# Two transformer blocks on one core: the rests of the ordinary weight tiles from ScalarE and an accumulating DMA instead of VectorE

## The chip, the cores and the metric

One Trainium2 chip, one core. The core's engines run side by side, each through its own list of instructions in order, and wait for each other through semaphores: TensorE (PE) multiplies, VectorE (DVE), ScalarE (ACT) and GpSimd (POOL) work elementwise, SyncE (SP) issues most of the DMAs; 16 DMA engines move the data. The metric is the device time of one execution in microseconds (us); lower is better.

## The reference

Two layers, one after the other, on 512 tokens of width 1024, all in f32. Cut to the large products:

```python
def first_block(x, c, ...):
    mod = silu_c @ ada_w[l] + ada_b[l]
    h = rms_norm(h_res, norm_pre_w[l]) * (1.0 + scale) + shift
    z = h @ w_in[l]                          # 1024 -> 6144
    u_pool, g_pool, q, f_pre, i_in, g_h = jnp.split(z, ...)
    pool_out = multiscale_pool(u_pool, pool_w[l], pool_scale[l]) * jax.nn.silu(g_pool)
    o = hgrn2_chunkwise(q, log_f, k, i_in)
    y = jnp.concatenate([pool_out, hgrn_out], axis=-1) @ w_out[l]
    h_res = h_res + gate * rms_norm(y, norm_post_w[l])
...
def hybrid_layer(x, norm_g, w_in, ...):
    proj = rms_norm_2(x, norm_g) @ w_in      # 1024 -> 11208
    y_a = chunked_spatial_gating(...); y_b = dsa_attention(...)
    y_c = short_gated_conv(...);       y_d = forgetting_attention(...)
    branch_d = jnp.einsum('nbsw,nwd->bsnd', ys, w_branch)
    merged = jnp.sum(jax.nn.sigmoid(gates) * branch_d, axis=2)
    return x + merged @ w_out
```

Each weight is read once from DRAM, and nearly all of the arithmetic is products of the 512 tokens with a weight.

## The kernel before

**Products in three parts.** TensorE multiplies in a rounded f32 format (f32r). To keep the precision, an operand is split into a rounded part and a rest: `whi` and `wlo` for a weight, `HH` and `HL` for the tokens. A product is three products, `HH·whi + HH·wlo + HL·whi`, in one PSUM bank; the list of each tile begins with `whi`, and the first product with `wlo` comes second or third (`mm3`, line 334). One product of 128x128 with 128x512 follows the last after about 0.23 us.

**Weight tiles.** The packed weights `wts` are loaded by SP, 1 MB at a time (two tiles of 128x1024), into the three raw buffers (`dma_raw`, line 237), and near the end also into groups of slots of 128x512. `pump` (line 280) splits the next tile: ScalarE rounds it into `whi` (line 308), VectorE subtracts `whi` from the raw weights and writes `wlo` (line 309). When both tiles of a raw buffer are split, the buffer is free (`used`, line 253) and SP's next load is issued. There are 188 tiles in the ring:

- eight `s` tiles at the start (896 columns),
- 42 `P` tiles (`P1n2_0` and the like) in the last quarter, products of a Strassen scheme, whose weights are sums made in the buffers (`prep`, line 263),
- 138 ordinary tiles: `q3`, `i0_0`, `f4`, `u0`, `gp0`, `ki`, `dq0`, `gt0_1_0`, `wb2_0_0` and so on. Each is read by 24 products, some 5.4 us of TensorE; a `P` tile by 12, some 2.7 us.

**The ring.** `whi` and `wlo` have three buffers each (`WB = 3`), used in turn, and a tile is asked for two tiles ahead (`LA = 2`). So the split of a tile can begin when the tile three places earlier has had its last product, and has to end when the two tiles between them are done. Between two tiles the side work puts its own products (`hgrn`, `topk`, `fox`, `dsa`: attention and scans, stepped by `run`, line 817).

**What sets the order.** A scheduler orders each engine's list at build time from priorities; the splits have high priority (line 305). On the chip the lists are fixed, and each engine takes its instructions in that order. Eight startup steps (to line 543) are ordered by hand on VectorE and ScalarE. ScalarE also evaluates all functions and copies most banks out (helper `act`, line 110). GpSimd has only `HL` at the start (line 522), a factor per `f` tile (line 568) and the running sums of the pooling windows, up to four chained additions for each `u` tile (lines 915 to 921); after the first 330 us it is nearly empty. Before the change it issues no DMA. At the two last steps of a branch in the last quarter come the `wb` tiles: `P7n2_0`, `P7n2_1`, `wb2_1_0`, `wb2_1_1`, then `P2`, `P4`, `wb2_0_0`, `wb2_0_1`, the same for branches 3 and 1.

Of the kernel before, what the change touches and what calls it, by code (L numbers as in the profile page):

```python
# [13 lines left out]
AF = mybir.ActivationFunctionType  # L14
ALU = mybir.AluOpType
# [73 lines left out]
def kernel(  # L89
# [15 lines left out]
    V, A, G, T = nc.vector, nc.scalar, nc.gpsimd, nc.tensor  # L105
# [23 lines left out]
    def get():  # L129
        assert free_slots, "out of slots"  # L130
        s = Slot(free_slots.popleft())
        low[0] = min(low[0], len(free_slots))
        return s
# [7 lines left out]
    def bget():  # L141
        assert banks, "out of banks"
        return banks.popleft()
# [40 lines left out]
    whi = [const.tile([128, 1024], F32R, name=f"whi{i}") for i in range(WB)]  # L184
    wlo = [const.tile([128, 1024], F32R, name=f"wlo{i}") for i in range(WB)]
# [4 lines left out]
    for r, items in enumerate(raws):  # L190
        o = 0
        for name, w in items:
            if name[0] == "B":
                quarter[name[1:]] = r
                n, q = name[1:].split("_")
# [9 lines left out]
    n = 0  # L205
# [27 lines left out]
    def width(w, *bufs):  # L233

        return w if all(b.t is not None for b in bufs) else 512
# [17 lines left out]
    def used(r):  # L253
        left[r] -= 1
        if left[r] == 0:
            b = raw_b.pop(r)
            if ws["dma"] >= len(raws) and b.s:
                put(*b.s)
            else:
                pool.append(b)  # L260
                dma_raw()

    def prep(i):

        if i >= len(flat) or flat[i][0][0] != "P":
            return
        p, n, j = flat[i][0][1], flat[i][0][3], int(flat[i][0][5])
        args = {"5": ("11", "12"), "6": ("11", "22"), "7": ("12", "22"), "4": ("11", "21")}.get(p)
        if args is None:
            return  # L270
        rd, ra = (quarter[f"{n}_{q}"] for q in args)
        d, a_ = raw_b[rd], raw_b[ra]
        w = width(1024, d, a_)
        for o in range(j * 1024, (j + 1) * 1024, w):
            with tc.high_priority():
                V.tensor_sub(d.at(o, w), a_.at(o, w), d.at(o, w))
        if p in "74":
            used(ra)

    def pump(upto):  # L280
        while ws["split"] <= min(upto, len(flat) - 1):
            i = ws["split"]
            name, r, o, w = flat[i]
            if i in in_slots:
                hs, ls = [get(), get()], [get(), get()]
                for kk in range(2):
                    src = raw_b[r].at(o + kk * 512, 512)
                    with tc.high_priority():
                        A.activation(hs[kk].r, src, AF.Copy)
                        V.tensor_sub(ls[kk].r, src, hs[kk].r)  # L290
                in_slots[i] = hs, ls
                used(r)
                ws["split"] += 1
                continue
            if i not in split_ids:
                if i >= ws["next"]:
                    return
                ws["split"] += 1
                continue
            while ws["prep"] <= i + 1:  # L300
                prep(ws["prep"])
                ws["prep"] += 1
            s = split_ids[i] % WB
            b = raw_b[r]
            with tc.high_priority():
                n = width(w, b)
                for c in range(0, w, n):
                    A.activation(whi[s][:, c:c + n], b.at(o + c, n), AF.Copy)  # L308
                    V.tensor_sub(wlo[s][:, c:c + n], b.at(o + c, n), whi[s][:, c:c + n])  # L309
            used(r)  # L310
            ws["split"] += 1

    def wget(name, ahead=LA):
        i = ws["next"]
        assert flat[i][0] == name, (flat[i][0], name)
        ws["next"] += 1
        pump(i + ahead)
        if i in in_slots:
            return in_slots[i]
        s = split_ids[i] % WB  # L320
        return whi[s], wlo[s]
# [109 lines left out]
    for h in range(2):  # L431
        r = slice(32 * h, 32 * h + 1)
# [4 lines left out]
    for h in range(2):  # L437
        r = slice(32 * h, 32 * h + 1)
# [55 lines left out]
    for k in range(8):  # L494
# [3 lines left out]
        for i in range(1, 4):  # L498
# [4 lines left out]
        V.tensor_scalar(S1[:, kc], md[:, 1:2], B1[:, kc], PV[:, PV_NPW + k:PV_NPW + k + 1],  # L503
                        op0=ALU.add, op1=ALU.mult)
        pump(k)
        xk = xnT[k].f if k else xb[0][:]
        if k == 0:
# [685 lines left out]
    w = {}  # L1193
    first = ws["next"]
    for t in range(NT):
        norm_T(t)
        b = bget()
        ts_ = slice(t * 128, (t + 1) * 128)
        for j in range(4):
            if t == 0:  # L1200
                w[j] = wget(f"av_{j}", first + 3 - ws["next"])
            wh, wl = w[j]
            for kk in range(2):
                k = 2 * j + kk
                c = slice(kk * 512, (kk + 1) * 512)
                h, l = (wh[:, c], wl[:, c]) if j < 3 else (wh[kk].r, wl[kk].r)
                mm(b[:], HH[:, k, ts_], h, k == 0, False)
                mm(b[:], HH[:, k, ts_], l, False, False)
                mm(b[:], HL[:, k, ts_], h, False, k == 7)
            if t == NT - 1:  # L1210
                if j == 3:
                    put(*wh, *wl)
                else:
                    pump(first + 4 + j)
        s = get()
        act(s.f, b[:], AF.Copy)
        bput(b)
        avt.append(s)
# [720 lines left out]
    n = BRANCHES[0]  # L1939
# [173 lines left out]
```

## Time and profile before

| | |
|---|---|
| median of 3 runs | 1121.67 us (1121.64 to 1124.52) |
| the profiled execution, its own time | 1124.12 us |
| its span, first to last instruction | 1121.9 us |
| TensorE busy | 1099.9 us, 98% of the span |
| VectorE busy | 801.7 us, 71% |
| ScalarE busy | 627.6 us, 56% |
| GpSimd busy | 64.9 us, 6% |
| DMA | 122.76 MB, mean 109 GB/s |

Busy time counts an engine's own instructions; TensorE's are pipelined, so that they overlap. The chain of work that ended last is followed back from the last instruction and says at each step which engine the next step waited for. A wait names the instruction that ended it. The granted clock of TensorE has two levels, 1.2 and 2.4 GHz, shown as 0.5 and 1.0.

### The profile page before, as it was taken

The numbers are of one execution on the slowest core, as the hardware profiler recorded it, in microseconds if no ns is written. First come the engines' busy times: TensorE is split into PE (matmuls) and PEld (weight loads), VectorE is DVE, ScalarE is ACT, GpSimd is POOL, SyncE is SP. The second block draws the span as 40 slices with busy tenths as digits, with TensorE's granted clock in tenths as the row PEclk, the third lists the DMA queues.
The fourth block names the chain that finished last, engine by engine and source line by source line (L and its number), as shares of the span: only waits on it lengthen the run. The fifth ranks groups of instructions, "written<-read, shape, count | busy, mean of one in ns | idle before, by whom it ended". The sixth has DMA issues, their size and how long they took to land.

```text
span 1121.9 us, 14034 instructions
## 1 busy us (share of the span) xinstructions
PE 1099.9 (98%) x5213; PEld 912.5 (81%) x5213; DVE 801.7 (71%) x1604; ACT 627.6 (56%) x1005; POOL 64.9 (6%) x73
## 2 busy tenths in 40 slices
PE   6999999999999999999999999999999999999997
PEld 5788888888878888788888888888888888888885
DVE  7978788764778645889798754655756958797735
ACT  6595497955578464554245634565653545545513
POOL 1330210100420000000000000000000000000000
PEclk9999999999989999999999999999999999999999
DMA  9734223232122253232322222222232342335102
GB/s 332 280 131 165 76 95 131 76 113 79 72 76 76 95 201 118 95 113 85 129 87 84 77 93 105 75 76 75 75 104 92 108 157 85 113 113 189 56 1 76
DMA packets 31617, 122.76 MB, mean 109 GB/s; under 512 B 3638, under 2 KB 3894, under 8 KB 21308
## 3 DMA queue, kind: packets, MB, share of 16 engines
q1 hardware_dynamic: 30972, 120.81, 30.6%
q10 hardware_dynamic: 576, 1.05, 0.3%
q8 instruction: 41, 0.67, 0.2%
q14 instruction: 28, 0.23, 0.1%
HBM read 117.64 MB, written 4.20 MB: 109 GB/s over the span
## 4 chain that ended last, share of the span: by engine, by line
PE 81%; DVE 8%; DMA 3%; ACT 3%; issue 3%; POOL 2%; SPq 0%; POOLq 0%; DVEq 0%; ACTq 0%
PE bank L332 80%; DMA slot<-in_adw_dram 2%; DVE slot L1349 1%; ACT slot L110 1%; DVE best L1348 1%; ACT L110 1%; POOL slot L916 1%; ACT whi L308 1%; DVE slot L358 1%; DVE wlo L309 1%; PE bank L1397 1%; POOL slot L915 1%; DMA raw<-in_wts_dram 1%; DVE slot L490 1%; DMA slot<-in_x_dram 1%
## 5 line engine op out<-in xcount | busy, mean ns | idle before, releaser
L308 ACT ACTIVATE whi<-raw 128x1024 fp32r<-128x1024 f32 (+1 forms) x164 | 172.4, 1052 | 233.9 <-PE bank L332 204.0
L309 DVE TENSOR_TENSOR wlo<-raw,whi 128x1024 fp32r<-128x1024 f32 (+1 forms) x164 | 199.1, 1214 | 114.2 <-ACT whi L308 106.5
L332 PE MATMUL bank<-HH,whi 128*128 128x512 f32 x704 | 272.8, 397 | 1.2 <-ACT HH L110 1.0
L332 PE MATMUL bank<-HH,wlo 128*128 128x512 f32 x704 | 268.7, 392 | 0.0
L332 PE MATMUL bank<-HL,whi 128*128 128x512 f32 x704 | 267.7, 391 | 0.0
L332 PE MATMUL bank<-whi,slot 128*128 128x512 f32 x644 | 203.8, 391 | 0.0
L110 ACT ACTIVATE slot<-bank 128x512 f32<-128x512 f32 (+7 forms) x281 | 131.1, 496 | 59.6 <-PE bank L332 27.3
L110 ACT ACTIVATE slot<-slot 128x512 fp32r<-128x512 f32 (+4 forms) x194 | 109.1, 591 | 86.5 <-DVE slot L1960 20.0
L332 PEld LDWEIGHTS bank<-HH,whi 128*128 128x128 f32 x704 | 132.3, 189 | 30.6 <-ACT HH L110 4.2
L332 PEld LDWEIGHTS bank<-HH,wlo 128*128 128x128 f32 x704 | 132.7, 188 | 28.4
L332 PEld LDWEIGHTS bank<-HL,whi 128*128 128x128 f32 x704 | 132.9, 189 | 26.6
L332 PEld LDWEIGHTS bank<-whi,slot 128*128 128x128 f32 x644 | 120.9, 188 | 25.4 <-DVE slot L358 0.2
L332 PE MATMUL bank<-slot,slot 128*128 128x128 f32 (+5 forms) x748 | 131.7, 319 | 3.9 <-ACT slot L110 3.9
L332 PE MATMUL bank<-wlo,slot 128*128 128x512 f32 x328 | 127.8, 390 | 0.0
L332 PEld LDWEIGHTS bank<-slot,slot 128*128 128x128 f32 (+2 forms) x748 | 108.9, 186 | 19.1 <-issue 4.1
L110 ACT ACT_TABLE_LOAD x86 | 110.3, 1283 | 5.5 <-PE bank L332 2.7
L332 PE MATMUL bank<-whi,HL 128*128 128x512 f32 x280 | 109.4, 391 | 1.4 <-DVE HL L358 1.3
L332 PE MATMUL bank<-whi,HH 128*128 128x512 f32 x280 | 109.9, 393 | 0.6 <-ACT slot L110 0.4
L332 PE MATMUL bank<-wlo,HH 128*128 128x512 f32 x280 | 109.1, 390 | 0.0
L332 PEld LDWEIGHTS bank<-wlo,slot 128*128 128x128 f32 x328 | 61.6, 188 | 12.6
L332 PEld LDWEIGHTS bank<-whi,HL 128*128 128x128 f32 x280 | 52.6, 188 | 13.0 <-DVE HL L358 2.0
L332 PEld LDWEIGHTS bank<-whi,HH 128*128 128x128 f32 x280 | 52.6, 188 | 12.1 <-ACT slot L110 0.9
(229 smaller groups left out, 1123.9 us busy)
## 6 DMA issues: line engine op xcount, KB each, us to landing
raw<-in_wts_dram SPq DMA_DIRECT2D x80, 1024.0 KB, 4.8
slot<-in_wts_dram SPq DMA_DIRECT2D x36, 256.0 KB, 3.2
slot<-in_adw_dram SPq DMA_DIRECT2D x32, 256.0 KB, 6.3
slot<-in_x_dram SPq DMA_DIRECT2D x16, 256.0 KB, 4.1
raw<-in_wts_dram SPq DMA_DIRECT2D x8, 448.0 KB, 6.1
slot<-in_rows_dram SPq DMA_DIRECT2D x11, 256.0 KB, 3.8
XD<-slot SPq DMA_DIRECT2D x8, 256.0 KB, 2.0
slot<-XD SPq DMA_DIRECT2D x7, 256.0 KB, 4.6
```

The source lines that it names most:

```text
L110: return A.activation(o, i, func, **kw)
L308: A.activation(whi[s][:, c:c + n], b.at(o + c, n), AF.Copy)
L309: V.tensor_sub(wlo[s][:, c:c + n], b.at(o + c, n), whi[s][:, c:c + n])
L332: T.matmul(o, l, r, start=start, stop=stop, **kw)
L358: V.tensor_sub(dst_l, src, dst_h)
L490: V.tensor_tensor_reduce(junk[i % 2].f, ada[k][i].f, cb[i % 2].f, 1.0, 0.0, ALU.mult, ALU.add, mds[k][:, i:i + 1])
L915: G.tensor_copy(d.f[:, 0:sh], src.f[:, 0:sh])
L916: G.tensor_add(d.f[:, sh:512], src.f[:, sh:512], src.f[:, 0:512 - sh])
L1348: V.max(best, sc.f[:, 0:n])
L1349: V.match_replace(sc.f[:, 0:n], best, sc.f[:, 0:n], MARK)
L1397: T.transpose(tb[:, cs], P[u1].f[:, cs], IDENT)
```

## The change

For all tiles whose name doesn't begin with `P` or `s`, VectorE's subtraction goes away. ScalarE writes the negative of the rounded part into `wlo`, and a DMA issued by GpSimd reads the tile's weights a second time from DRAM and adds them to what stands in `wlo`. For the eight tiles that lie in slots, ScalarE writes two halves and one DMA adds the whole tile.

```diff
                 for c in range(0, w, n):
                     A.activation(whi[s][:, c:c + n], b.at(o + c, n), AF.Copy)
-                    V.tensor_sub(wlo[s][:, c:c + n], b.at(o + c, n), whi[s][:, c:c + n])
+                    if name[0] in "Ps":
+                        V.tensor_sub(wlo[s][:, c:c + n], b.at(o + c, n), whi[s][:, c:c + n])
+                    else:
+                        A.activation(wlo[s][:, c:c + n], whi[s][:, c:c + n], AF.Copy, scale=-1.0)
+                if name[0] not in "Ps":
+                    G.dma_start(wlo[s][:, 0:w], wts[r, :, o:o + w], accum_op=ALU.add)
             used(r)
```

Lines after 314 stand five lower in the changed kernel: 915 and 916 become 920 and 921. 138 tiles move (130 split in one piece of 128x1024, eight in two halves), and 138 DMAs of 512 KB stand newly in GpSimd's list.

ScalarE at the first ordinary tiles, `q3` (`whi_118`) and `i0_0` (`whi_116`), right behind the startup; before:

```order
L308 ACTIVATE whi_118<-raw_114 128x1024
L308 ACTIVATE whi_116<-raw_114 128x1024
L110 ACT_TABLE_LOAD
L110 ACTIVATE SM<-PV 128x8
L110 ACT_TABLE_LOAD
```

and after:

```order
L308 ACTIVATE whi_118<-raw_114 128x1024
L308 ACTIVATE whi_116<-raw_114 128x1024
L312 ACTIVATE wlo_121<-whi_118 128x1024
L312 ACTIVATE wlo_119<-whi_116 128x1024
L308 ACTIVATE whi_117<-raw_115 128x1024
L110 ACT_TABLE_LOAD
```

The negation of `q3` stands behind the rounding of both tiles, and no longer beside it on another engine.

ScalarE at `wb2_0_0` (`whi_118`), which follows two `P4` tiles (`whi_116`, `whi_117`) in the last quarter; before:

```order
L308 ACTIVATE whi_116<-raw_113 128x1024
L308 ACTIVATE whi_117<-raw_113 128x1024
L110 ACTIVATE slot_7304<-slot_4810 128x512
L308 ACTIVATE whi_118<-raw_115 128x1024
L110 ACTIVATE slot_6899<-slot_6899 128x512
L110 ACTIVATE slot_6901<-slot_6901 128x512
L308 ACTIVATE whi_116<-raw_115 128x1024
```

and after:

```order
L308 ACTIVATE whi_117<-raw_113 128x1024
L110 ACTIVATE slot_7430<-slot_4892 128x512
L308 ACTIVATE whi_118<-raw_115 128x1024
L110 ACTIVATE slot_7021<-slot_7021 128x512
L312 ACTIVATE wlo_121<-whi_118 128x1024
L110 ACTIVATE slot_7023<-slot_7023 128x512
L308 ACTIVATE whi_116<-raw_115 128x1024
L312 ACTIVATE wlo_119<-whi_116 128x1024
```

Between the rounding and the negation one more function of 128x512 stands in the list.

GpSimd at the running sums of the last pooling tile `u7`, four chained additions; before:

```order
L916 TENSOR_TENSOR slot_2540<-slot_2538 128x511
L915 COPY slot_2543<-slot_2540 128x2
L916 TENSOR_TENSOR slot_2543<-slot_2540 128x510
L915 COPY slot_2546<-slot_2543 128x4
L916 TENSOR_TENSOR slot_2546<-slot_2543 128x508
```

and after:

```order
L921 TENSOR_TENSOR slot_2580<-slot_2578 128x511
L920 COPY slot_2583<-slot_2580 128x2
L921 TENSOR_TENSOR slot_2583<-slot_2580 128x510
L314 DMA wlo_119<-in_wts_dram 128x1024
L920 COPY slot_2586<-slot_2583 128x4
L921 TENSOR_TENSOR slot_2586<-slot_2583 128x508
```

One of the new DMAs stands inside the chain.

## Rows read from the trace of the kernel before

**Rows 1.** The page, busy us (share of the span) and instructions of the engines.

```profile
PE 1099.9 (98%) x5213; PEld 912.5 (81%) x5213; DVE 801.7 (71%) x1604; ACT 627.6 (56%) x1005; POOL 64.9 (6%) x73
```

**Rows 2.** The page, shares by engine of the chain that ended last.

```profile
PE 81%; DVE 8%; DMA 3%; ACT 3%; issue 3%; POOL 2%; SPq 0%; POOLq 0%; DVEq 0%; ACTq 0%
```

**Rows 3.** Groups by shape: line, engine, tiles, count | busy us, mean ns | idle before, releaser.

```profile
L309 DVE TENSOR_TENSOR wlo<-raw,whi 128x1024 fp32r<-128x1024 f32 x156 | 190.4, 1221 | 114.2 <-ACT whi L308 106.5 <-PE bank L332 5.4 <-PE bank L1397 1.2
L308 ACT ACTIVATE whi<-raw 128x1024 fp32r<-128x1024 f32 x156 | 164.8, 1057 | 233.2 <-PE bank L332 204.0 <-issue 22.5 <-DVE slot L1801 2.1
...
L308 ACT ACTIVATE whi<-slot 128x512 fp32r<-128x512 f32 x48 | 30.3, 631 | 33.2 <-PE bank L332 28.5 <-issue 3.2 <-DVE wlo L309 0.7
```

**Rows 4.** Waits: who <- for whom: us in total, times, longest.

```profile
ACT whi L308 <- PE bank L332: 232.6, 118, 5.1
```

**Rows 5.** DMA issues: tiles, queue, count, KB each, median us to landing; queue's totals.

```profile
q1 hardware_dynamic: 30972, 120.81, 30.6%
...
raw<-in_wts_dram SPq DMA_DIRECT2D x80, 1024.0 KB, 4.8
...
slot<-in_adw_dram SPq DMA_DIRECT2D x32, 256.0 KB, 6.3
...
raw<-in_wts_dram SPq DMA_DIRECT2D x1, 512.0 KB, 4.0
```

**Rows 6.** Timeline, ScalarE and TensorE at `cc1`: start us, us, instruction [idle before].

```profile
674.06 1.06 ACT L308 ACTIVATE whi<-raw 128x1024 fp32r<-128x1024 f32 x1 [3.17 <-PE bank L332]
...
686.43 0.39 PE L332 MATMUL bank<-HH,wlo 128*128 128x512 f32 x1
```

**Rows 7.** Timeline, ScalarE and TensorE at `q3` (and `i0_0`).

```profile
56.85 1.99 ACT L308 ACTIVATE whi<-raw 128x1024 fp32r<-128x1024 f32 x2
...
59.99 0.39 PE L332 MATMUL bank<-HH,wlo 128*128 128x512 f32 x1
```

**Rows 8.** Timeline, ScalarE and TensorE at `ki`.

```profile
478.21 1.06 ACT L308 ACTIVATE whi<-raw 128x1024 fp32r<-128x1024 f32 x1 [0.41 <-PE bank L332]
...
482.60 0.39 PE L332 MATMUL bank<-HH,wlo 128*128 128x512 f32 x1
```

**Rows 9.** Timeline, ScalarE and TensorE at `i1_0`.

```profile
230.08 1.05 ACT L308 ACTIVATE whi<-raw 128x1024 fp32r<-128x1024 f32 x1
...
236.51 0.39 PE L332 MATMUL bank<-wlo,HH 128*128 128x512 f32 x1
```

**Rows 10.** Timeline, ScalarE and TensorE at `wb2_0_0`.

```profile
931.12 1.06 ACT L308 ACTIVATE whi<-raw 128x1024 fp32r<-128x1024 f32 x1 [0.52 <-PE bank L332]
932.08 1.14 ACT L110 ACTIVATE slot<-slot 128x512 f32<-128x512 f32 x2
...
936.53 0.39 PE L332 MATMUL bank<-wlo,slot 128*128 128x512 f32 x1
```

**Rows 11.** Windows (us): busy PE, PEld, DVE, ACT, POOL (counts), PEclk, DMA share, GB/s.

```profile
322.00:324.00 2.00, 0.56 (x3) 0.12 (x1) 1.02 (x2) 0.72 (x2) 0.87 (x2) 1.00 0.00 0
325.00:331.00 6.00, 5.84 (x13) 4.27 (x14) 6.00 (x14) 4.31 (x7) 0.00 (x0) 0.50 0.00 0
460.00:462.00 2.00, 0.67 (x3) 0.41 (x3) 2.00 (x10) 0.50 (x3) 0.00 (x0) 1.00 0.12 43
```

**Rows 12.** Timeline, GpSimd and TensorE at 321 to 327 us, TensorE at 461 us.

```profile
321.39 1.26 POOL L916 TENSOR_TENSOR slot<-slot 128x504 f32<-128x504 f32 x1
...
324.33 1.37 PE L332 MATMUL bank<-slot,ONES 128*128 128x512 f32 x2 [1.77 <-DVE slot L358]
...
326.47 0.63 PE L332 MATMUL bank<-HH,whi 128*128 128x512 f32 x1
...
461.55 0.50 PE L332 MATMUL bank<-whi,HL 128*128 128x512 f32 x1 [1.33 <-DVE HL L358]
```

**Rows 13.** Windows, columns as in Rows 11: the scans of the first block, and behind them.

```profile
160.00:240.00 80.00, 79.95 (x410) 67.14 (x410) 63.33 (x134) 68.19 (x99) 6.76 (x4) 1.00 0.29 99
240.00:320.00 80.00, 80.00 (x414) 67.68 (x413) 45.88 (x87) 42.51 (x63) 20.81 (x29) 1.00 0.26 92
```

## The prediction

> **What bounds the kernel now.** First the busy times: TensorE has 98% of the span, VectorE 71%, ScalarE 56%, GpSimd 6% [rows 1]. Since pipelined products overlap, 98% alone proves little, so next the chain that ended last: 81% of it is TensorE, 8% VectorE, 3% ScalarE [rows 2]. The reader is to see that VectorE, which the change relieves, holds up little. The waits say the same from the other side: 118 times, 232.6 us in all, ScalarE stands before the rounding of a weight tile and waits for TensorE to give back a buffer [rows 4]. The splits are made as soon as the ring lets them, and TensorE is late, not they. So time can be lost here much more easily than won: every microsecond that a `wlo` comes after TensorE's first product with it is lost whole.
>
> The quantity that decides is therefore the margin of a tile: from the end of its rounding to TensorE's first product with its `wlo`. For a tile in the middle, `cc1`, the rounding ends at 674.06 + 1.06 = 675.12 and the product starts at 686.43, a margin of 11.3 us [rows 6]. VectorE used 1.22 us of it [rows 3].
>
> **What is removed and what it is worth.** 130 subtractions of 1.221 us and 16 halves, taken at half of that, leave VectorE: 130 x 1.221 + 16 x 0.61 = 168 us of its 801.7 [rows 1, 3]. Where VectorE ends a wait of TensorE, in the rows 1.77 us and 1.33 us [rows 12], the first came behind GpSimd's sums and the second in the first block's end, with no weight tile in the way. I count 1 us gained, at most 3.
>
> **What is added: ScalarE.** 130 x 1.057 + 16 x 0.631 = 147.5 us [rows 3], so it goes from 627.6 to 775 us, 69% of the span. It lies on the path in two ways. One is the tile's own latency, below. The other is the first block's scans: from 160 to 240 us ScalarE is busy 68.19 of 80 us [rows 13]; eleven ordinary tiles are split there, which is 11.6 us more, 79.8 of 80. It recovers behind it (42.51 of 80 from 240 to 320 [rows 13]), and the margins there are long, so the price lies between 0 and 8 us; I take 3.
>
> **What is added: the DMA's latency.** No row shows an accumulating DMA, nor any DMA issued by GpSimd. Call D the time from the end of the negation to the landing. It reads 512 KB from DRAM, reads 512 KB of `wlo` and writes 512 KB. From below: one plain load of 512 KB lands after 4.0 us [rows 5], and an accumulating one has no reason to be quicker. The nearest row by bytes read is the load of 1024 KB, 4.8 us [rows 5]. GpSimd has to issue it, which I put at the size of one of its own instructions, 1.26 us at the longest [rows 12], 1.0 as an estimate. That is D = 5.8. From above: loads of 256 KB that share the engines with many others take 6.3 us [rows 5], with 1.26 and some 0.2 for semaphores 7.8 us. I take 5.8, and keep 4.0 and 7.8.
>
> The trace has the same volume twice as slow only for plain loads. The Trainium skill ("Collectives: The Full Stack", the section on the bandwidth ceiling) says that a reducing transfer reads two sources and so runs at half the rate of a copy; that agrees with taking the 1024 KB row and speaks against this change. It also has a fit for DMAs from GpSimd ("DMA: Bandwidth & Descriptors", Anatomy of one DMA): 2.0 us and the bytes at 436 GB/s, an estimate of 3.2 us for 512 KB; with D = 3.2 the sum below would be about 12 us instead of 46. No run here shows either.
>
> **The sum over the ring.** After the change a tile needs, from the end of its rounding, 1.06 us for the negation and D, together 6.9 us. A margin like that of `cc1`, 11.3 us, hides it and keeps 4.4. The following don't:
> - `q3`: its rounding is one of the pair that ends at 58.84, its product with `wlo` starts at 59.99 [rows 7]; by the order the negation comes behind both roundings. 58.84 + 1.06 + 5.8 = 65.7: 5.7 us late.
> - `ki`: 478.21 + 1.06 + 1.06 + 5.8 = 486.1 against 482.60 [rows 8]: 3.5 us.
> - `i1_0`: 230.08 + 1.05, then a copy of a bank that now stands between (0.57 us as in [rows 10]), 1.06 and 5.8 = 238.6 against 236.51 [rows 9]: 2.1 us.
> - `wb2_0_0`, behind two short `P` tiles: 931.12 + 1.06, one function of 0.57, 1.06 and 5.8 = 939.6 against 936.53 [rows 10]: 3.1 us. The margin is 4.35 us. There are two more like it (`wb3_1_0`, `wb1_1_0`): 9.3 us in all.
> - `wb2_1_0` and `wb3_0_0` lie in slots; their last half needs 0.43 us less for the negation and has some 0.5 us more of margin, 2.2 us each: 4.4. The sixth such tile, `wb1_0_0`, has transposes in front and more room.
>
> Sum 5.7 + 3.5 + 2.1 + 9.3 + 4.4 = 25.0 us. The second tile of each pair has the delay of the first as extra margin and adds nothing.
>
> **TensorE's clock.** The one fall in the middle of the trace follows a gap of 1.77 us: TensorE ran 0.56 of 2 us from 322 to 324, and from 325 to 331 the granted clock is 0.50, its lower level, 1.2 GHz [rows 11, 12]; a product takes 0.63 us there [rows 12]. Six microseconds at half speed lose 3.0. A gap of 1.33 us, with TensorE busy 0.67 of 2 us, left the clock at 1.00 [rows 11, 12]. The eight gaps above are 2.1 to 5.7 us long. I take six falls, 18 us; the bounds are none and eight, 0 and 24.
>
> **GpSimd's list.** It is in order. The DMA of a tile waits for ScalarE's negation, and behind it stand the factors of the `f` tiles and the sums of the `u` tiles. By the order the DMAs stand mostly before a tile's sums start. One stands inside the chain of `u7`, whose last addition ends at 322.65 and which held up TensorE until 324.33 [rows 12]: 1 us more, between 0 and 3 if it waits too. SP's queue gets nothing new; raw buffers are freed a little earlier, since VectorE no longer reads them.
>
> Together 25 + 18 + 3 + 1 - 1 = **46 us**. The profiled execution took 1124.12 us on a span of 1121.9, 2.2 us around it, and lies 2.45 us above the median; the forecast is against the median: 1121.67 + 46 = 1167.7, **1168 us**.
>
> **The ends.** With D = 4.0 the sites give 3.9 + 1.7 + 0.3 + 3.9 + 0.8 = 10.6, one or two falls 5, the rest 3: 1140. With D = 7.8 every site has 2 us more and four smaller ones join (4 us): 25 + 16 + 4 = 45, eight falls 24, ScalarE and GpSimd 10: 1201.
>
> **Rivals.**
> 1. *Cheap DMA.* The accumulate lands like a plain load or earlier, D of 3 to 4.3. Then only `q3`, `ki` and a little of the `wb` tiles is seen: 1127 to 1145. For it: the engines are used 30.6% by the load queue [rows 5]. Against it: two reads and a queue that has not been used. Chance 0.18.
> 2. *Dear DMA.* The end of a rounding that frees a raw buffer also starts a load of 1 MB, so that every second accumulate shares the engines with one; 120.81 MB took 30.6% of them [rows 5], and 138 x 0.524 = 72 MB more with two reads each take another 18 to 37%. With D = 9 the eight sites have 3.2 us more than in the sum, 25 + 26 = 51 us, eight falls 24, the smaller sites 10, ScalarE and GpSimd 5: 90 us, 1212. Near D = 10.2 the margin of `cc1` is used up (11.3 less 1.06), and from there each microsecond is paid at every tile like it; with some forty of the 138 and 1 us, 1260. Chance 0.14.
> 3. *Faster.* The relief of VectorE is worth more than I count, and D is under 3 us, so that nothing in the ring stalls except 1 us at `q3`. VectorE's 8% of the chain are 90 us [rows 2], but TensorE runs beside most of it: the idle time that VectorE ends is only some 3 to 5 us. The point from which it decides is D = 3; the time is 1117. Chance 0.05.
> 4. *No difference*: D about 3 and the gain and the loss cancel, within 0.3% (3.4 us), about what a measurement of this kernel can tell from no change. Chance 0.05.
>
> The forecast, stalls at eight to ten tiles and the clock behind them, 1145 to 1210, has 0.58.
>
> **How the numbers follow.** Slower takes the forecast and rivals 1 and 2: 0.90; same 0.05; faster 0.05. The range has to reach into both neighbours: 1130 leaves out the two that lie below and a small part of the cheap case (0.12), 1225 the dearer half of the dear case (0.08).
>
> **What the profile after would show.** VectorE near 634 us, ScalarE near 775. In the list of DMA issues a new row for line 314, 138 times, 512 KB, with D less the wait: between 4 and 8 us, and its median settles the largest term. In the waits TensorE before products with `wlo`, ended by that DMA, 5 us and more at `q3`, 2 to 4 us at `ki` and the five `wb` tiles, and none in the plain stretches from 640 to 870 us. The granted clock at 0.50 behind most of them. ScalarE nearly full from 160 to 240 us. I am wrong on the side of too much if TensorE's waits for the DMA sum to under 10 us, on the side of too little if they come at plain tiles such as `cc1`, or if GpSimd's sums wait behind DMAs for more than 3 us.

## The result, and the profile after

The changed kernel takes 1193.28 us (median of 4 runs, 1191.06 to 1195.6) where the kernel before took 1122.22 us on the same chip (1121.64 to 1124.52): a ratio of 1.0629, 95% interval 1.0603 to 1.0656, so slower by 71 us. The forecast was 1168, slower by 46, with a range up to 1225. The direction and the mechanism came as written; the size of several terms did not.

The page of the changed kernel, busy us (share of the span) and instructions of each engine; the chain that ended last, by engine; two DMA queues (packets, MB, share of the engines' time); and two rows of DMA issues (KB each, median us to landing):

```profile
PE 1119.1 (94%) x5213; PEld 922.6 (77%) x5213; DVE 655.0 (55%) x1458; ACT 758.4 (64%) x1154; POOL 176.4 (15%) x211
...
q0 software_dynamic: 19872, 72.36, 34.2%
q1 hardware_dynamic: 30972, 120.81, 29.4%
...
PE 67%; issue 10%; DMA 9%; ACT 7%; DVE 6%; POOL 1%; SPq 0%; POOLq 0%; ACTq 0%; DVEq 0%
...
raw<-in_wts_dram SPq DMA_DIRECT2D x80, 1024.0 KB, 5.4
wlo<-in_wts_dram POOLq DMA_DIRECT2D x138, 512.0 KB, 5.8
```

Against [rows 1, 2, 5] TensorE's share of the chain has gone from 81% to 67%, and DMA's from 3% to 9%. The 72 MB of the new queue (q0) hold the engines longer than the 121 MB of the loads (q1). The waits of the same kernel (who <- for whom: us in total, times, longest):

```profile
PE bank L337 <- DMA wlo<-in_wts_dram: 45.3, 13, 7.5
DVE slot L363 <- ACT slot L110: 59.2, 35, 8.4
```

The first row did not exist before: TensorE stands 13 times, 3.5 us on average, before a product with a `wlo` that has not landed. The second was 12.1 us, 10 times, before (line 363 was 358): VectorE, which has less to do, stands before ScalarE more often. What of that reaches TensorE comes further below.

Where the time went can be read from the start of the same product in both traces. The timeline of the changed kernel, TensorE's first product with the `wlo` of `q3`, `wh1_0`, `ki`, `cc1`, `wb2_0_0`, `wb2_0_1` and `wb1_1_0` (start us, us, instruction, idle before):

```profile
67.90 0.80 PE L337 MATMUL bank<-HH,wlo 128*128 128x512 f32 x1 [7.47 <-DMA wlo<-in_wts_dram]
...
443.76 0.79 PE L337 MATMUL bank<-wlo,slot 128*128 128x512 f32 x1 [5.48 <-DMA wlo<-in_wts_dram]
...
518.20 0.80 PE L337 MATMUL bank<-HH,wlo 128*128 128x512 f32 x1 [4.03 <-DMA wlo<-in_wts_dram]
...
725.11 0.39 PE L337 MATMUL bank<-HH,wlo 128*128 128x512 f32 x1
...
985.87 0.50 PE L337 MATMUL bank<-wlo,slot 128*128 128x512 f32 x1 [1.70 <-DMA wlo<-in_wts_dram]
...
992.47 0.50 PE L337 MATMUL bank<-wlo,slot 128*128 128x512 f32 x1 [1.50 <-DMA wlo<-in_wts_dram]
...
1103.76 0.79 PE L337 MATMUL bank<-wlo,slot 128*128 128x512 f32 x1 [6.67 <-DMA wlo<-in_wts_dram]
```

`q3` started at 59.99, `ki` at 482.60, `cc1` at 686.43, `wb2_0_0` at 936.53 [rows 6 to 8, 10]. So the delay is 7.9 us at `q3`, 35.6 at `ki`, 38.7 at `cc1`, 49.3 at `wb2_0_0` and 71.9 at the end of the span (1193.8 against 1121.9). Between `ki` and `cc1`, a stretch of 32 tiles that all use the new way, only 3.1 us are lost, about what the lower clock just behind `ki` costs. The loss is made in a few places.

The issues of the accumulating DMA on GpSimd for five of these, `wh1_0`, `ki`, `cc1`, `wb2_0_0` and `wb1_1_0`:

```profile
433.72 0.87 POOL L314 DMA_DIRECT2D wlo<-in_wts_dram  x1 [8.72 <-ACT wlo L312]
...
511.13 0.86 POOL L314 DMA_DIRECT2D wlo<-in_wts_dram  x1 [45.07 <-ACT wlo L312]
...
715.59 0.86 POOL L314 DMA_DIRECT2D wlo<-in_wts_dram  x1 [4.58 <-ACT wlo L312]
...
980.73 0.86 POOL L314 DMA_DIRECT2D wlo<-in_wts_dram  x1 [27.03 <-PE bank L337]
...
1093.61 0.86 POOL L314 DMA_DIRECT2D wlo<-in_wts_dram  x1 [41.73 <-PE bank L337]
```

At `cc1` the product starts 9.5 us after the issue and waits for nothing. Where TensorE waits, its start is the landing: 5.1 us after the issue at `wb2_0_0`, 7.1 at `ki`, and 10.0 and 10.2 at `wh1_0` and `wb1_1_0`; the last three are over the 5.8 us of the median. The same DMA is nearly twice as slow in some of the places where it is waited for.

Summed over the trace, the steps between two products that are over 0.25 us longer than such a step usually is make 71.5 us, against 14.4 us before: 57 us of new stalls. Products at the lower clock follow each other after 0.43 us and not 0.23; there are 75 such steps in its stretches, against 12 before: 12.6 us. Together 70 of the 72 us.

### The profile page after: what moved, and what is told of

The parts are those of the page before. It is cut to its first block, busy times and chain, and to the rows that moved or that the text cites. A ratio compares the mean times of both kernels' runs of the same rounds, so it can differ in the third digit from the quotient of the medians.

```text
span 1193.8 us, 14332 instructions
## 1 busy us (share of the span) xinstructions
PE 1119.1 (94%) x5213; PEld 922.6 (77%) x5213; DVE 655.0 (55%) x1458; ACT 758.4 (64%) x1154; POOL 176.4 (15%) x211
## 3 DMA queue, kind: packets, MB, share of 16 engines
q0 software_dynamic: 19872, 72.36, 34.2%
## 4 chain that ended last, share of the span: by engine, by line
PE 67%; issue 10%; DMA 9%; ACT 7%; DVE 6%; POOL 1%; SPq 0%; POOLq 0%; ACTq 0%; DVEq 0%
PE bank L337 66%; DMA wlo<-in_wts_dram 6%; ACT L110 2%; ACT slot L110 2%; DMA raw<-in_wts_dram 1%; ACT whi L308 1%; ACT wlo L312 1%; DMA slot<-in_adw_dram 1%; DVE slot L495 1%; PE bank L1402 1%; DMA slot<-in_x_dram 0%; DVE slot L559 0%; DVE slot L363 0%; DVE slot L693 0%; DVE slot L1155 0%
## 5 line engine op out<-in xcount | busy, mean ns | idle before, releaser
L314 POOL DMA_DIRECT2D wlo<-in_wts_dram x138 | 119.9, 870 | 891.8 <-ACT wlo L312 554.8
L337 PE MATMUL bank<-whi,slot 128*128 128x512 f32 x644 | 209.8, 401 | 0.0
L337 PE MATMUL bank<-wlo,slot 128*128 128x512 f32 x328 | 133.1, 406 | 29.5 <-DMA wlo<-in_wts_dram 28.4
L110 ACT ACTIVATE slot<-bank 128x512 f32<-128x512 f32 (+7 forms) x281 | 133.8, 494 | 30.2 <-PE bank L337 19.6
L312 ACT ACTIVATE wlo<-whi 128x1024 fp32r<-128x1024 f32 (+1 forms) x146 | 146.3, 1004 | 0.9
L337 PEld LDWEIGHTS bank<-whi,slot 128*128 128x128 f32 x644 | 125.3, 195 | 26.8 <-DVE slot L363 0.2
L337 PEld LDWEIGHTS bank<-wlo,slot 128*128 128x128 f32 x328 | 64.1, 196 | 46.4 <-DMA wlo<-in_wts_dram 21.1
L363 DVE TENSOR_TENSOR slot<-slot,slot 128x512 fp32r<-128x512 f32 x74 | 51.2, 701 | 48.5 <-ACT slot L110 33.9
```

Of the source, the lines that this page charges most:

```text
L110: return A.activation(o, i, func, **kw)
L312: A.activation(wlo[s][:, c:c + n], whi[s][:, c:c + n], AF.Copy, scale=-1.0)
L314: G.dma_start(wlo[s][:, 0:w], wts[r, :, o:o + w], accum_op=ALU.add)
L337: T.matmul(o, l, r, start=start, stop=stop, **kw)
L363: V.tensor_sub(dst_l, src, dst_h)
```

## The experiments

Two theories stood first. **L**, the forecast's: the rest lands too late at a few tiles with short margins, and the clock falls behind the long stalls. **S** and **T**: the change loads ScalarE (S) or the DMA engines and SBUF (T), and this slows the kernel everywhere. All kernels of one group ran beside the kernel before on the same chip, which took 1122.95 to 1123.18 us.

### Is it a few tiles?

The tiles are the fourteen whose product with `wlo` follows the landing within 0.2 us in the changed kernel. They alone by the new way:

```diff
-                    if name[0] in "Ps":
+                    if name not in TIGHT:
...
-                if name[0] not in "Ps":
+                if name in TIGHT:
```

> The reverse: only those 14 tiles get negation and accumulating DMA, the other 124 stay with VectorE as before the change. Theory L: TensorE still waits at most of the 14. Where a second accumulate shared the engines the landing gets shorter (from 7.5 to 12.3 us towards the 5.2 to 5.5 us of one alone), so the stalls shrink from some 45 to 25 to 35 us, and four to six falls of the clock cost 12 to 20: 1155 to 1177 us. Rival S and rival T: a tenth of the negations and of the traffic, a tenth of 71 us: 1127 to 1132 us.

1181.58 us, ratio 1.0522 (1.0505 to 1.0539): a tenth of the tiles brings 58 of the 71 us, a little more than L's upper end, and far from S and T. The waits of this kernel, and its DMA issues:

```profile
PE bank L340 <- DMA wlo<-in_wts_dram: 40.0, 13, 8.0
```

```profile
wlo<-in_wts_dram POOLq DMA_DIRECT2D x14, 512.0 KB, 7.7
```

I had expected the landing to shorten where the neighbours' accumulates are gone. It hardly did: the median of the fourteen is 7.7 us, against 8.4 at the same tiles of the changed kernel, and the longest wait, at `q3`, is 8.0. So it is not mainly the accumulates that slow each other there. The exception is `f5`: its landing falls from 10.5 to 5.1 us, and TensorE no longer waits for it.

The reverse, the same fourteen back on VectorE and the other 124 by the new way:

```diff
-                    if name[0] in "Ps":
+                    if name[0] in "Ps" or name in TIGHT:
...
-                if name[0] not in "Ps":
+                if name[0] not in "Ps" and name not in TIGHT:
```

> The 14 tiles at which TensorE waited for the new DMA in the changed kernel (q3, f5, i1_0, i1_1, wh1_0, ki, wb2_1_0, wb2_0_0, wb2_0_1, wb3_1_0, wb3_1_1, wb3_0_0, wb1_1_0, wb1_0_0) get their rest from VectorE again, as before the change; the other 124 keep negation and accumulating DMA. Theory L (the time is lost at the few tiles whose DMA lands after TensorE wants them, and in the clock behind them): nearly all of the 71 us goes, no wait of TensorE for a DMA over 1 us, no fall of the clock but the two of the kernel before; what stays is ScalarE's full stretch from 190 to 220 us, 0 to 9 us, so 1122 to 1131 us. Rival S (ScalarE's 147 us of negations hold the kernel up at many places): nine tenths of them are still there, 1170 to 1190 us. Rival T (72 MB more traffic slow the loads and SBUF everywhere): the same, 1160 to 1190 us.

1155.28 us, ratio 1.0282 (1.0263 to 1.0300). More than half of the loss is gone, but 32 us stay, which L had not expected. Its waits, and its longest one in the timeline:

```profile
PE bank L340 <- DMA wlo<-in_wts_dram: 15.7, 8, 4.3
```

```profile
435.59 0.80 PE L340 MATMUL bank<-wlo,slot 128*128 128x512 f32 x1 [4.26 <-DMA wlo<-in_wts_dram]
```

This wait is at `wh0_1`, the tile behind `wh1_0`. While `wh1_0` was late, its delay was margin for `wh0_1`; with `wh1_0` early, `wh0_1` is the late one. The tight thing is the bunch, not the tile. So a third kernel puts whole bunches back, 36 tiles, and leaves 102:

```diff
-                    if name[0] in "Ps":
+                    if name.startswith(tuple(OLD)):
...
-                if name[0] not in "Ps":
+                if not name.startswith(tuple(OLD)):
```

> Whole bunches go back to VectorE, not single tiles: the s and P tiles, q3, i0_0, i0_1, gp3, pw0, f4 to f7, q4 to q7, the four i1, the four wh, ki, qi0, qi1 and all wb of branches 2, 3 and 1 (36 of the 138 ordinary tiles); the other 102 keep negation and DMA. Theory L (late landing where splits come in bunches): the 17 us of TensorE's waits for the DMA that were left with 14 tiles on VectorE had moved to the next tile of the same bunch (i1_2, wh0_1, qi0, wb1_1_1), so they go now, and with them the falls of the clock; ScalarE's share, 11.7 us with all 138 negations, shrinks too: 1123 to 1131 us. Rival S (ScalarE or traffic, spread evenly): three quarters of what the change costs remain, 1165 to 1180 us.

1128.16 us, ratio 1.0045 (1.0030 to 1.0060): with three quarters of the DMAs still there, 66 of the 71 us are back. TensorE waits for none of them, and the clock falls only at the two places where it fell before. And the plain stretch alone, 61 tiles from `au0` to `wb0_0_1`:

```diff
-                    if name[0] in "Ps":
+                    if not name.startswith(tuple(NEW)):
...
-                if name[0] not in "Ps":
+                if name.startswith(tuple(NEW)):
```

> The new way only for the 61 tiles from au0 to wb0_0_1 (some 525 to 920 us), where splits come one at a time and margins are 10 to 18 us; all others as before the change. Theory L: a landing 5 to 9 us after the negation is hidden; up to 3 us from functions of ScalarE that stand behind a negation: 1121 to 1126 us. If the relief of VectorE is worth something anywhere, the time falls below 1120 us. Rival T (traffic slows TensorE or the loads): 61 of 138 DMAs, so over 1140 us.

1124.32 us, ratio 1.0016 (1.0007 to 1.0026). That stretch in this kernel and, under it, in the changed one and in the kernel before (window, us; busy us of PE, PEld, DVE, ACT, POOL with counts; clock; DMA share; GB/s):

```profile
525.00:930.00 405.00, 403.08 (x1910) 336.21 (x1908) 220.16 (x518) 254.89 (x398) 47.06 (x55) 1.00 0.69 165
```

```profile
525.00:930.00 405.00, 403.08 (x1921) 336.66 (x1920) 215.74 (x523) 262.82 (x408) 52.84 (x61) 1.00 0.72 169
```

```profile
525.00:930.00 405.00, 404.22 (x1915) 337.44 (x1914) 278.48 (x578) 204.82 (x344) 0.00 (x0) 1.00 0.27 94
```

TensorE is busy 403.08 of 405 us in the first two, with the DMA engines used 69 to 72% of the time, and 404.22 before. Where tiles come one at a time the new way costs about 1 us. It wins nothing: some 60 us less work on VectorE in that stretch brought no time.

### What of ScalarE, and of the traffic?

ScalarE alone: it negates as in the changed kernel, and VectorE adds the raw weights to that, so that there is no DMA.

```diff
                         A.activation(wlo[s][:, c:c + n], whi[s][:, c:c + n], AF.Copy, scale=-1.0)
+                        V.tensor_add(wlo[s][:, c:c + n], b.at(o + c, n), wlo[s][:, c:c + n])
-                if name[0] not in "Ps":
-                    G.dma_start(wlo[s][:, 0:w], wts[r, :, o:o + w], accum_op=ALU.add)
```

> ScalarE alone: it writes the negated rounded part into wlo for all 138 tiles as in the changed kernel, and VectorE adds the raw weights to it (no DMA, GpSimd as before). Each rest comes one negation, 1.06 us, later than before the change, and ScalarE has its full 147 us more. Theory L: only margins under 1 us are felt, at q3 about 1 us and perhaps i1_0, and the full stretch of ScalarE from 160 to 240 us costs 3 to 9 us: 1124 to 1133 us, no new fall of the clock. Rival S: most of the 71 us is here, 1170 us or more.

1134.87 us, ratio 1.0104 (1.0089 to 1.0119): 11.7 us, above the 3 to 9 that were named, and far below S. Two windows of this kernel, the first block's scans, and from behind `q3` to 525 us; under it the second one in the kernel before:

```profile
160.00:240.00 80.00, 78.33 (x402) 65.51 (x401) 58.50 (x121) 78.71 (x103) 11.18 (x4) 1.00 0.28 99
...
69.00:525.00 456.00, 444.97 (x2196) 369.82 (x2195) 328.85 (x662) 348.90 (x519) 52.59 (x57) 1.00 0.30 103
```

```profile
69.00:525.00 456.00, 452.24 (x2232) 376.98 (x2231) 334.70 (x680) 287.48 (x452) 46.49 (x55) 0.99 0.30 106
```

TensorE is busy 7.3 us less between 69 and 525 us. From 160 to 240 us ScalarE is full, 78.71 of 80 us, and TensorE is busy 1.6 us less than before, 78.33 against 79.95 [rows 13]; most of the rest is strewn over the first block in pieces of one to two microseconds. Part of it is latency and not load, since every rest comes 1.06 us later: at `q3` TensorE waits 1.0 us for VectorE's addition.

The traffic alone: VectorE makes all rests, and GpSimd adds 448 KB of each tile's weights to a spare tile that nobody reads.

```diff
                     V.tensor_sub(wlo[s][:, c:c + n], b.at(o + c, n), whi[s][:, c:c + n])
+                if name[0] not in "Ps":
+                    G.tensor_copy(SPARE[:, 0:1], whi[s][:, w - 1:w])
+                    G.dma_start(SPARE, wts[r, :, o:o + 896], accum_op=ALU.add)
```

> The traffic alone: VectorE makes all rests as before the change, and beside it GpSimd issues at each of the 138 tiles, behind the rounding, an accumulating DMA of 448 KB of the same weights into a spare tile that nobody reads (a copy of one column paces it; the one spare tile lets only one such DMA run at a time). Theory L: the traffic itself costs next to nothing, 1121 to 1127 us, of which up to 4 us may come from GpSimd's running sums standing behind a DMA that waits for the one before it. Rival T (traffic and port contention): 63 of 72 MB are moved, so most of the 71 us: over 1165 us.

1175.33 us, ratio 1.0464 (1.0447 to 1.0482): by the total L fails here and T is right. The profile says that the number is not the traffic's. Waits of this kernel, and two windows:

```profile
POOL SPARE L313 <- DMA SPARE<-in_wts_dram: 559.0, 110, 9.4
...
ACT whi L310 <- POOL SPARE L313: 68.0, 21, 6.6
...
DVE slot L902 <- POOL slot L926: 42.6, 7, 17.6
```

```profile
69.00:525.00 456.00, 412.36 (x2012) 342.84 (x2012) 298.43 (x606) 265.34 (x420) 138.45 (x171) 0.96 0.61 151
525.00:930.00 405.00, 404.07 (x1924) 337.35 (x1923) 284.29 (x605) 207.16 (x347) 74.02 (x124) 1.00 0.69 164
```

With one spare tile GpSimd waits in its list for each DMA's landing, 110 times; the running sums of the pooling stand behind that, and VectorE waits up to 17.6 us for them. The next rounding into the same `whi` waits for GpSimd's copy of one column, too, 21 times. I had put up to 4 us on it. The loss of TensorE, 40 us more than before, lies in the first block, where those sums are. From 525 to 930 us GpSimd does the same without sums, at 164 GB/s, and TensorE is busy 404.07 of 405. So the traffic itself costs next to nothing there (404.22 before); for the first block this kernel shows nothing. It shows what a wait inside GpSimd's list costs, which the changed kernel avoids, as it has three buffers.

### What makes the DMA long in the bunches?

Two kernels change the transfer, not the order. One copies without adding (the rest is then the raw weights, the sum is left out); one adds only the first 256 columns of each tile, a quarter of the bytes (the other three quarters of a rest stay the negated part).

```diff
-                    G.dma_start(wlo[s][:, 0:w], wts[r, :, o:o + w], accum_op=ALU.add)
+                    G.dma_start(wlo[s][:, 0:w], wts[r, :, o:o + w])
```

> As the changed kernel, but the DMA does not add: it copies the 512 KB of raw weights over the negated part (the sum is left out, wlo holds the raw weights). Same queue, same issue, same waits, one read less. If the second read costs what the prediction took it for (the landing of a plain load of 512 KB is 4.0 us, that of the accumulate 5.8): median landing 4 to 4.6 us, stalls of some 10 to 20 us fewer with their clock, 1155 to 1175 us. If the adding costs nothing: 5.5 us and more, 1188 to 1198 us.

```diff
-                    G.dma_start(wlo[s][:, 0:w], wts[r, :, o:o + w], accum_op=ALU.add)
+                    G.dma_start(wlo[s][:, 0:256], wts[r, :, o:o + 256], accum_op=ALU.add)
```

> As the changed kernel, but the DMA adds only the first 256 of a tile's 1024 columns (128 KB instead of 512; the other three quarters of a rest stay the negated rounded part, so this part of the computation is left out). Theory L: the landing time is bytes and the sharing of the engines: alone it falls from 5.2 to some 3 us, in bunches from 7.5 to 12 to 4 to 6 us. TensorE waits still about 3 us at q3 and 1 us at ki and the wb tiles, and the 11.7 us of the negations stay: 1137 to 1152 us. Rival F (a fixed cost of the queue, GpSimd's issue and completion): the median stays above 5 us, and the time above 1170 us.

The plain copy: 1167.67 us, ratio 1.0397 (1.0367 to 1.0426), inside what the second read would give. The quarter: 1161.05 us (1153.91 to 1165.38), ratio 1.0329 (1.0289 to 1.0369), dearer than L's 1137 to 1152, and under the 1170 of a fixed cost. The tile `wlo` in the changed kernel and in the plain copy (GpSimd's issue, ns min/median/max and first and last start; from the issue to the landing), then its landing in the quarter:

```profile
L314 POOL DMA_DIRECT2D wlo<-in_wts_dram x138: 856/865/1021, 60.4 to 1148.0; - x138
...
DMA to landing us min/median/max: 5.1/5.8/12.3
```

```profile
L314 POOL DMA_DIRECT2D wlo<-in_wts_dram x138: 530/530/709, 61.1 to 1120.0; - x138
...
DMA to landing us min/median/max: 3.3/4.4/8.2
```

```profile
DMA to landing us min/median/max: 3.1/3.5/7.5
```

And the page's row of GpSimd's queue, of the plain copy:

```profile
q0 software_dynamic: 19872, 72.36, 18.8%
```

The same 72.36 MB hold the engines 34.2% of 1193.8 us when they are added, 408 us, and 18.8% of 1165.8 us when they are copied, 219 us: 1.86 times. The Trainium skill ("Collectives: The Full Stack", the section on the bandwidth ceiling) gives half the rate of a copy for a reducing transfer in a collective, since it reads two sources; these rows, of a DMA outside any collective, agree with 1.86. Its fit for DMAs from GpSimd ("DMA: Bandwidth & Descriptors", Anatomy of one DMA), an estimate of 3.2 us for 512 KB, is met by the fastest plain copy, 3.3 us, but not by any accumulate, whose fastest took 5.1.

TensorE's waits for these DMAs, 45.3 us in the changed kernel, in the plain copy and under it in the quarter:

```profile
PE bank L337 <- DMA wlo<-in_wts_dram: 24.3, 9, 7.6
```

```profile
PE bank L337 <- DMA wlo<-in_wts_dram: 15.5, 9, 4.5
```

Bytes and adding explain the lower ends, and a large part of the waits: from the issue to the landing `wh1_0` goes from 10.0 us to 5.9 in the plain copy, `wb1_1_0` from 10.1 to 6.1. They do not explain all of the upper ends: even 128 KB take up to 7.5 us, and `q3` waits for the plain copy as long as for the accumulate, and 4.49 us for the quarter, in these rows of the two timelines:

```profile
68.73 0.79 PE L337 MATMUL bank<-HH,wlo 128*128 128x512 f32 x1 [7.60 <-DMA wlo<-in_wts_dram]
```

```profile
64.77 0.76 PE L337 MATMUL bank<-HH,wlo 128*128 128x512 f32 x1 [4.49 <-DMA wlo<-in_wts_dram]
```

So something else fills the engines there as well. In the changed kernel the rounding, not the DMA, is the last reader of a raw buffer, so that SP's next load of 1 MB can start before the accumulate is issued. The next kernel reads the raw buffer in place of DRAM, so that the load cannot start before the accumulates have landed:

```diff
-                    G.dma_start(wlo[s][:, 0:w], wts[r, :, o:o + w], accum_op=ALU.add)
+                    for c in range(0, w, n):
+                        G.dma_start(wlo[s][:, c:c + n], b.at(o + c, n), accum_op=ALU.add)
```

> As the changed kernel, but the accumulating DMA reads the raw weights from the raw buffer in SBUF and not a second time from DRAM (two halves where they lie in slots). So the raw buffer is free, and SP's next load of 1 MB starts, only when both accumulates of its tiles have landed: the loads no longer share the engines with them. Theory X (loads beside the accumulates stretch the landing in the bunches): the first accumulate of a bunch lands after 5.0 to 5.5 us instead of 7 to 10 (f5, wh1_0, wb2_1_0, wb3_0_0, wb1_1_0), the second still after 7 to 9; TensorE's waits fall by 15 to 25 us with two or three falls of the clock: 1155 to 1178 us. Rival Y (the accumulates slow each other, loads don't matter): landings as in the changed kernel, and loads come later on top: 1190 us or more.

1170.37 us, ratio 1.0419 (1.0394 to 1.0445), 23 us under the changed kernel, as X said and not Y. Its longest waits in the timeline, at `q3` and at `wh0_1`:

```profile
65.16 0.80 PE L338 MATMUL bank<-HH,wlo 128*128 128x512 f32 x1 [4.75 <-DMA wlo<-raw]
...
445.84 0.79 PE L338 MATMUL bank<-wlo,slot 128*128 128x512 f32 x1 [4.80 <-DMA wlo<-raw]
```

All its waits for these DMAs, and the landings of the tile `wlo`:

```profile
PE bank L338 <- DMA wlo<-raw: 22.6, 12, 4.8
```

```profile
DMA to landing us min/median/max: 3.3/5.2/11.7
```

The waits halve, 45.3 to 22.6 us (and 2.6 more in the tiles in slots). The wait at `q3` goes from 7.47 to 4.75 us, with the same neighbours among the accumulates. `wh1_0` no longer waits; the wait of 4.80 us is at the tile behind it, whose accumulate runs beside a load and the next accumulate, so again the bunch only passes it on. The reading has a limit: reading from SBUF is also quicker by itself (median 5.2 against 5.8 us), so not all of the 23 us are the loads'. And the plain copy cut the waits as much, to 24.3 us, with all loads in place. At `q3` the plain copy saved nothing and moving the load away saved 2.7 us; there the accumulate's first packet moves 2.8 us after the issue in the changed kernel, behind the load's, and 1.6 us after it in this one.

What lengthens the landing at the other tiles can be counted from the packets in the trace of the changed kernel. Of the 10.0 us from issue to landing at `wh1_0`, packets of SP's queue take 5.2 us of the engines' time (the time of the packets, shared out over the 16 engines) and those of the accumulates 3.1. At `f5`, `ki`, `wb2_1_0`, `wb3_0_0` and `wb1_1_0` it is 4.3 to 6.4 us against 2.8 to 4.4. At `wb1_0_0`, which lands after 5.2 us, SP's queue moves nothing in between. So at these six tiles it is mostly the loads that make a landing of 5 us one of 7 to 10. At `wb2_0_1` and `wb3_1_1`, the seconds of their pairs, the other accumulate adds some 2 us.

### A version that is faster than both

The kernel before had one stall of its own, 1.77 us behind GpSimd's sums of `u7`, and a fall of the clock behind it [rows 11, 12]. With nothing of the change in it, only those sums go to VectorE:

```diff
+                E = V if i == 7 else G
-                G.tensor_copy(d.f[:, 0:sh], src.f[:, 0:sh])
-                G.tensor_add(d.f[:, sh:512], src.f[:, sh:512], src.f[:, 0:512 - sh])
+                E.tensor_copy(d.f[:, 0:sh], src.f[:, 0:sh])
+                E.tensor_add(d.f[:, sh:512], src.f[:, sh:512], src.f[:, 0:512 - sh])
...
-            G.tensor_mul(src.f[:, 0:16], src.f[:, 0:16], CORR[:, g * 16:(g + 1) * 16])
+            (V if i == 7 else G).tensor_mul(src.f[:, 0:16], src.f[:, 0:16], CORR[:, g * 16:(g + 1) * 16])
```

> The kernel before the change, with nothing of the change in it; only the nine operations of the running sums of the last pooling tile u7 go from GpSimd to VectorE. In the trace of before they end a wait of TensorE of 1.77 us and a fall of the clock of 6.8 us stands behind it. If both belong to that chain: 1.8 us and 3.4 us of half speed and about 1 us of the small waits behind, so 4 to 7 us less, 1115 to 1119 us, and no fall of the clock before the end. If VectorE is late then with what stands behind the sums, or the next wait takes the place: within 2 us of before.

1118.04 us, ratio 0.9958 (0.9946 to 0.9971): 4.9 us faster than before. The window of that place, and the last addition on VectorE, which took 1.26 us on GpSimd [rows 12]:

```profile
313.00:325.00 12.00, 12.00 (x69) 10.41 (x68) 11.34 (x29) 9.54 (x19) 0.00 (x0) 1.00 0.23 83
```

```profile
320.65 0.68 DVE L917 TENSOR_TENSOR slot<-slot 128x504 f32<-128x504 f32 x1
```

TensorE is busy throughout at the full clock, and VectorE, at 11.34 of 12 us, had the room without the change. The 1.77 us of the stall are under half of the gain; the others are the small waits behind it and the lower clock. How much is the clock's differs between executions. In the profile of the kernel with the plain stretch alone, no fall followed the same wait:

```profile
324.81 1.08 PE L340 MATMUL bank<-slot,ONES 128*128 128x512 f32 x2 [1.78 <-DVE slot L366]
...
325.00:332.00 7.00, 6.46 (x27) 4.87 (x27) 7.00 (x17) 5.31 (x8) 0.00 (x0) 1.00 0.00 0
```

And the two executions of the kernel before that had the highest mean clock beside this run, 0.998 and 0.999, took 1121.98 and 1122.54 us, still some 4 us more than the kernel with the sums on VectorE. So the clock is probably the smaller part of the gain.

## Why the prediction came out as it did

**What bounds the kernel: right.** TensorE bounds it, VectorE's relief is worth nothing (the plain stretch alone came within 0.3%), and the margin of a tile decides. `cc1`, with its 11.3 us, waits for nothing. VectorE is busy 655 us where 634 were forecast, since instructions that overlap count once; nothing hung on it.

**D, the latency: right as a median, wrong where it mattered.** I reckoned 1.0 us for the issue and a landing behind it, 5.8 us in all; measured from the end of the negation, as I had defined it, the median is 6.3, and 5.8 from the issue, which starts 0.29 us behind the negation (the sum had nothing for that, the upper bound 0.2 as an estimate without a row). The step that failed is using one D for all sites. It spreads from 5.4 to 12.6 us, and at ten of the fourteen tight tiles it lies between 7.3 and 10.8, because what makes a margin short also makes the engines full: two or three splits follow each other, and so two or three accumulates and the loads of 1 MB for which they freed a buffer run at once. By the packets the loads weigh most there, and the other accumulates at the seconds of two pairs. The prediction had the load beside the accumulate, but put it into the dear rival as a cost of every second tile, not of these sites.

**The ring's stalls: mostly the right places, 49 us and not 25.** Lost at each (steps longer than usual, less what was lost there before):

| tile | forecast | measured |
|---|---|---|
| `q3` | 5.7 | 7.6 |
| `ki` | 3.5 | 4.2 |
| `i1_0`, and `i1_1` behind it | 2.1 | 2.3 + 1.4 |
| `wb2_0_0`, `wb3_1_0`, and the seconds of their pairs | 3.1 + 3.1 | 1.9 + 1.9, and 1.7 + 1.6 |
| `wb1_1_0` | 3.1 | 6.8 |
| `wb2_1_0`, `wb3_0_0` (in slots) | 2.2 + 2.2 | 5.1 + 5.1 |
| `wb1_0_0` | 0 | 1.4 |
| `wh1_0` | not seen | 5.6 |
| `f5` | not seen | 2.2 |

With 5.1 us from issue to landing `wb2_0_0` comes in below its forecast, and with 10.2 us `wb1_1_0` far above. The step "the second tile of each pair adds nothing" is wrong: its DMA runs beside the first one's and lands later by more than the first's delay, at `wb2_0_1` by 1.50 us of waiting. `wh1_0` was not listed, since its margin before the change, 7.1 us, is a little longer than the 6.9 us that I reckoned with; with a landing 10.0 us after its issue it is among the dearest.

**The clock: right in kind, 13 us and not 18.** Six new falls were forecast, and six came, at `q3`, `wh1_0`, `ki`, `wb2_1_0`, `wb3_0_0` and `wb1_1_0`. Behind `wb1_1_0`, and at `q3` while it waits and behind it:

```profile
1104.00:1108.00 4.00, 4.00 (x10) 3.13 (x11) 0.00 (x0) 0.00 (x0) 0.00 (x0) 0.50 0.45 123
...
60.00:68.00 8.00, 0.53 (x3) 0.11 (x1) 0.00 (x0) 7.94 (x12) 3.89 (x4) 0.72 0.95 222
68.50:73.50 5.00, 5.00 (x13) 3.98 (x12) 0.00 (x0) 0.25 (x1) 3.05 (x2) 0.50 0.76 151
```

The mean of 0.72 from 60 to 68 us shows that the clock fell while TensorE still stood; that part of the time at half speed costs nothing. So a fall cost 2.1 us and not 3.0. Waits of 1.70 and 1.50 us at `wb2_0_0` and `wb2_0_1` brought none, those of 4.03 us and more all did (as did the 1.77 us of `u7` before the change, while the 1.78 us at the same place in the kernel with the plain stretch alone did not), so that I draw no bound from these.

**ScalarE: the full stretch right, the cost elsewhere.** 3 us (0 to 8) were forecast for the stretch from 160 to 240 us. With the negations alone ScalarE is busy 78.71 of 80 us there, as the 79.8 reckoned, and TensorE loses 1.6 us. But the negations cost 11.7 in all, one to two microseconds each in many places, most of them in the first block, and for those the sum had nothing. How much of that is load and how much the 1.06 us of latency stays open. In the changed kernel some 8 of the 57 us of stalls are not at the fourteen tiles; that these are ScalarE's is argued from its waits, not shown apart.

**GpSimd's list: right.** The stalls behind `u7` are 1 to 2 us longer than before (TensorE's waits there sum to 3.4 us against 1.9), where 1 was forecast, and no sum waits for a landing. **The total** came nearer than its terms: the stalls were 24 us over the forecast and ScalarE's part above it too, while the clock's 5 us went the other way. **Rivals:** the dear case was the nearer one; two of its parts, contention by the loads and long landings, are true, but were felt in the bunches only. Plain tiles hardly paid.

## What to carry to other kernels

A mean latency does not price a change; take the latency at the tight places, where transfers come together for the same reason for which the margins are short. Before an engine's work goes to a DMA, ask whether that engine ends any wait of the bound one: here it did not, and a hidden move was worth nothing. When one late tile is mended, look at the next of its bunch, since the first one's delay was its cover.

## What the runs showed of the hardware

- Adding into SBUF held the DMA engines 1.86 times as long as copying the same 72.36 MB, and its issue on GpSimd took 0.87 us against 0.53.
- Of an accumulating DMA the smallest landing was 5.1 us for 512 KB and 3.1 us for 128 KB: a quarter of the bytes saves 2 us. Among other transfers both took up to more than twice that, 12.3 and 7.5 us.
- At six of the tight tiles, where a 512 KB accumulate landed after 7.0 to 10.5 us, packets of SP's queue held the engines for 4.3 to 6.4 us of that.
- 1.8 times the traffic (169 against 94 GB/s from 525 to 930 us) cost TensorE about 1 of 405 us, although a load of 1 MB landed after 5.4 us against 4.8 (medians of the whole run); only what was waited for directly was felt.
- The same wait of TensorE, 1.77 and 1.78 us at the same place, was followed by a fall of the granted clock to 0.50 in one execution and by none in another.
